# A one-core decoder step: the groups' combination issued in two parts, and the sample's convolution ten taps at a time

## The chip, the cores and the metric

One core of a Trainium2 chip runs one launch. The metric is the device time of the launch in microseconds, the median of several runs. Five engines work side by side, each through its own queue in order: TensorE (PE, with its weight loads listed as PEld), VectorE (DVE), ScalarE (ACT), GpSimd (POOL) and SyncE (SP, which here only issues DMA transfers).

## The reference, cut to what matters

One layer for 1024 prompt tokens and 64 sample tokens (8 sequences of 8), with shared weights, all in float32:

```
h = x @ w_in + b_in                       # 1088 x 10240: conv value, conv gate, silu gates, q, k, v, merge gates
u = a_val * sigmoid(a_gate)               # 1024 channels
conv_raw[t] = sum_j conv_w[j] * u_hist[t + j]     # depthwise, 31 taps; u_hist starts with zeros (prompt)
                                                  # or with 30 stored columns per sequence (sample)
for g in 3 groups (window, dilation) = (128,1), (512,4), (2048,16):   # 8 heads of 64
    o_g, lse_g = dilated window attention with a distance penalty
attn = sum_g softmax_g(lse)[g] * o_g      # "the combination of the groups"
y = LayerNorm(ALPHA * x + W_out(sig(g_a) * W_a(swish(LN(conv_raw)) * silu(z_a)) + sig(g_b) * W_b(attn * silu(z_b))))
```

It also returns the new key, value and convolution buffers.

## The kernel before, in words

Each float32 matrix product is done as three products of high and low parts; `split` (L119 to L122) makes the parts of a weight row block on ACT (hi) and DVE (lo). Products come in chunks of 384, 352 and 352 columns (`proj_chunk`, L192), in one of three PSUM buffers named `mm`. The projection chunks are the bulk of PE's work.

Between them stand the attention *visits*. There are 12 units (f, g): a pair of heads f = 0..3 and a group g = 0..2; a unit is 4, 3 or 2 bursts, one burst a visit. In a visit PE does the transposes of the burst before (L386), the values of the burst before that (L410) and the scores of its own (L357). After the scores DVE adds the penalty and takes the row's extreme (L367), ACT takes the exponentials (L374), and the transposes of the next visit need these. `VISITS` says after how many projection chunks each visit comes. `tc.issue_after(done[0].ins)` puts PE's instructions of a block behind the last projection product traced so far; other engines' instructions in the block are not bound by it.

When the three units of a pair f are done, `combine(f, res)` (L451) joins them: two small POOL transfers bring the row statistics of groups 1 and 2 back (L455), some fifteen DVE operations on 128x16 and one ACT exponential give the weights `w` (L464 to L476); PE transposes `w` (L478), ACT copies it out of PSUM (L480), POOL writes it to DRAM (`wd`, L482) and reads it back spread over 64 partitions each (`wb`, six transfers, L487); then DVE multiplies the three outputs with `wb` and adds them (L489 to L492, five operations of 128x1024). For f = 0, 1, 2 this is called in one piece after the second visit of the next pair (g == 0, bi == 1); for f = 3 in the sample stage, after the first group of sample scores.

The convolution runs channel block by channel block (128 channels, c = 0..7; 0 to 4 beside the attention, 5 to 7 beside the sample stage). `conv_channels(c)` loads 30 stored columns per sequence into a sample buffer `us` (8 sequences x 38 columns; three such buffers take turns, c % 3), projects gate and value, and writes the gated product behind the stored columns (L520 on ACT, L525 on DVE), the prompt's into `ub` (two buffers, c % 2). `conv` then runs the 31 taps on DVE at low priority (LP): for each tap one operation of 128x1024 on the prompt (L541, L544) and one of 128x64 on the sample (L542, L546), both summed in place in one tile `acc` (slot 23, a single buffer), which goes to DRAM (`cvd`, L548). So ACT's write into `ub` of channel c waits for the last prompt tap of channel c-2.

The order of each engine's instructions is written at build time by a list planner: it goes by priority (visits +700, weight splits +1500, convolution -800, otherwise program order) and by its own estimate of when an instruction's inputs are there. At run time each engine follows that order and waits where an input is late.

Of the kernel before, what the change touches and what calls it, by code (L numbers as in the profile page):

```python
# [16 lines left out]
P = 128  # L17
# [3 lines left out]
NS = 64  # L21
# [23 lines left out]
def trunk_kernel(ctx, tc, I, O):  # L45
# [18 lines left out]
    def slot(i, shape, dt=F32, n="s"):  # L64
        return sp.tile(shape, dt, tag=f"S{i}", name=nm(n))
# [14 lines left out]
    def pt_ps():  # L80
        return psm.tile([P, 512], F32, tag="PT", bufs=2, name=nm("PT"))
# [369 lines left out]
    def combine(f, res):  # L451
        stn = tiny.tile([P, 3, 8, 4], F32, tag="stn", bufs=1, name=nm("stn"))
        dve.tensor_copy(out=stn[:, 0].rearrange("p t x -> p (t x)"), in_=res[0][1].rearrange("p t h x -> p (t h x)"))
        for g in (1, 2):
            pool.dma_start(out=stn[:, g], in_=res[g][1].rearrange("(t p) x -> p t x", p=P))  # L455

        nmax = stn.rearrange("p g t (h x) -> p g t h x", x=2)[:, :, :, :, 0]
        lsum = stn.rearrange("p g t (h x) -> p g t h x", x=2)[:, :, :, :, 1]
        mn = tiny.tile([P, 8, 2], F32, tag="mn", name=nm("mn"))
        e = tiny.tile([P, 3, 8, 2], F32, tag="e", bufs=1, name=nm("e"))  # L460
        el = tiny.tile([P, 3, 8, 2], F32, tag="el", bufs=1, name=nm("el"))
        den = tiny.tile([P, 8, 2], F32, tag="den", name=nm("den"))
        w = tiny.tile([P, 3, 2, 8], F32, tag="w", name=nm("w"))
        dve.tensor_tensor(out=mn, in0=nmax[:, 0], in1=nmax[:, 1], op=ALU.min)  # L464
        dve.tensor_tensor(out=mn, in0=mn, in1=nmax[:, 2], op=ALU.min)  # L465
        for g in range(3):
            dve.tensor_tensor(out=e[:, g], in0=mn, in1=nmax[:, g], op=ALU.subtract)
        ef = e.rearrange("p g t h -> p (g t h)")
        act.activation(out=ef, in_=ef, func=AF.Exp)
        for g in range(3):  # L470
            dve.tensor_tensor(out=el[:, g], in0=e[:, g], in1=lsum[:, g], op=ALU.mult)
        dve.tensor_tensor(out=den, in0=el[:, 0], in1=el[:, 1], op=ALU.add)
        dve.tensor_tensor(out=den, in0=den, in1=el[:, 2], op=ALU.add)
        dve.reciprocal(out=den, in_=den)
        for g in range(3):
            dve.tensor_tensor(out=w[:, g].rearrange("p h t -> p t h"), in0=e[:, g], in1=den, op=ALU.mult)  # L476
        pw = pt_ps()
        pe.transpose(pw[:48, :P], w.rearrange("p g h t -> p (g h t)"), ident)  # L478
        wt = half("PT", [48, P], 2)
        act.activation(out=wt, in_=pw[:48, :P], func=AF.Copy)  # L480
        wd = dram.tile([3, 2, NP_], F32, name=nm("wd"))
        pool.dma_start(out=wd.rearrange("g h (t p) -> (g h t) p", p=P), in_=wt)  # L482
        at = attn[f]
        for g in range(3):
            wb = slot(rotate("W", (12, 13)), [P, NP_], n="wb")
            for h in range(2):
                pool.dma_start(out=wb[64 * h:64 * h + 64, :], in_=wd[g, h:h + 1, :].to_broadcast([64, NP_]))  # L487
            if g == 0:
                dve.tensor_tensor(out=at[:, :NP_], in0=res[g][0], in1=wb, op=ALU.mult)  # L489
            else:  # L490
                dve.tensor_tensor(out=wb, in0=res[g][0], in1=wb, op=ALU.mult)
                dve.tensor_tensor(out=at[:, :NP_], in0=at[:, :NP_], in1=wb, op=ALU.add)  # L492


    PAD = 30
# [2 lines left out]
    def conv_channels(c):  # L498

        ub = slot(21 + c % 2, [P, PAD + NP_], n="ub")  # L500
        us = usv[c % 3]
        pool.memset(ub[:, :PAD], 0.0)
        sync.dma_start(out=us[:, :, :PAD], in_=I["state_conv"][c])
        wg = load_w(I["w_in"][F_AGATE + c], D)
        wv = load_w(I["w_in"][F_AVAL + c], D)
        b = b_sb[:, F_AVAL + c:F_AVAL + c + 1]
        bg = b_sb[:, F_AGATE + c:F_AGATE + c + 1]

        def spans(c0, cn):

            n = min(cn, NP_ - c0)
            out = [(slice(0, n), ub[:, PAD + c0:PAD + c0 + n], lambda a: a)]
            if n < cn:
                out.append((slice(n, cn), us[:, :, PAD:], lambda a: a.rearrange("p (b t) -> p b t", b=8)))
            return out

        for c0, cn in CHUNKS:
            ps = proj_chunk([(*wg, xhi, xlo)], c0, cn)
            for sl, dst, view in spans(c0, cn):
                act.activation(out=dst, in_=view(ps[:, sl]), func=AF.Sigmoid, bias=bg)  # L520
            yield
        for c0, cn in CHUNKS:
            ps = proj_chunk([(*wv, xhi, xlo)], c0, cn)
            for sl, dst, view in spans(c0, cn):
                dve.scalar_tensor_tensor(out=dst, in0=view(ps[:, sl]), scalar=b, in1=dst, op0=ALU.add, op1=ALU.mult)  # L525
            if c0 + cn < NT:
                yield
        pool.dma_start(out=O["convp"][c], in_=ub[:, NP_:])
        pool.dma_start(out=O["convs"][c], in_=us[:, :, 8:])
        with tc.high_priority(LP):  # L530
            conv(c, ub, us)
        yield

    def conv(c, ub, us):
        acc = slot(23, [P, NT], n="cv")
        accs = acc[:, NP_:].rearrange("p (b t) -> p b t", b=8)
        for j in range(31):
            w = convw[:, c, j:j + 1]
            if j == 0:
                cb = convb[:, c:c + 1]  # L540
                dve.tensor_scalar(out=acc[:, :NP_], in0=ub[:, :NP_], scalar1=w, scalar2=cb, op0=ALU.mult, op1=ALU.add)  # L541
                dve.tensor_scalar(out=accs, in0=us[:, :, :8], scalar1=w, scalar2=cb, op0=ALU.mult, op1=ALU.add)  # L542
            else:
                dve.scalar_tensor_tensor(out=acc[:, :NP_], in0=ub[:, j:j + NP_], scalar=w, in1=acc[:, :NP_],  # L544
                                         op0=ALU.mult, op1=ALU.add)
                dve.scalar_tensor_tensor(out=accs, in0=us[:, :, j:j + 8], scalar=w, in1=accs,  # L546
                                         op0=ALU.mult, op1=ALU.add)
        pool.dma_start(out=cvd[c], in_=acc)  # L548


    snew = dram.tile([3, 8, NS, NS], F32, name="snew")
# [45 lines left out]
    def beside():  # L597

        for g in range(3):
            yield from project_v(g)  # L600
            if g == 0:
                credit[1] = 1.7
            yield from project_qk(2 + g)
        keep[1] = slot(19, [P, NT], n="keep")
        usv.extend(keep[i][:, c:c + 304].rearrange("p (b t) -> p b t", b=8) for i, c in ((0, 12 * NS), (1, 0), (1, 304)))
        for c in range(5):
            for x in PAIRS[c]:
                yield from project_qk(x)
            yield from conv_channels(c)
# [4 lines left out]
    fill = beside()  # L614
    steps = 0
    n = 0
    for u, (f, g) in enumerate(units):
        if g == 0:
            res = []
        for bi, burst in enumerate(BURSTS[g]):  # L620
            n += 1

            while steps < (VISITS[n - 1] if n <= len(VISITS) else VISITS[-1] + 2.75 * (n - len(VISITS))) or (u not in qk):
                next(fill, None)
                steps += 1
            if bi == 0:
                q, k = qk[u]
                scr = None if g == 0 else dram.tile([NP_, 4], F32, name=nm("scr"))
                un, r = prompt_unit(f, g, q, k, scr)
                res.append(r)  # L630
            elif bi == 1:
                while ("v", g) not in ready:
                    next(fill, None)
                    steps += 1
                un["vt"] = load_v(f, g)
            with tc.issue_after(done[0].ins):
                visit({"unit": un, "tiles": burst})
                if bi == 0:
                    sample_new_scores(f, g, q, k)
            if todo and g == 0 and bi == 1:  # L640
                combine(*todo.pop())
        if g == 2:
            attn[f] = slot(14 + f, [P, NT], n="attn")
            todo.append((f, res))
# [195 lines left out]
    fill = filling()  # L840
    credit[1] = 0.0
    load_tiles()
    new = sample_queries(0)
    for pr in range(4):
        sc = sample_scores(*new)
        if pr < 3:
            new = sample_queries(pr + 1)
        if pr == 0:
            combine(*todo.pop())
            kvs[:0] = [9, 10, 11]  # L850
            odt += [slot(12 + i, [P, 2, 512], n="od") for i in range(2)]
        sample_values(pr, *sc)
# [311 lines left out]
```

## Time and profile before

| | |
|---|---|
| median of three runs | 1428.41 us (1426.35 to 1431.4) |
| the profiled execution | 1428.49 us, span 1426.7 us, clock 0.993 |
| PE busy | 1396.9 us, 98% |
| PEld busy | 1269.5 us, 89% |
| DVE busy | 845.2 us, 59% |
| ACT busy | 442.8 us, 31% |
| POOL busy | 184.6 us, 13% |

Busy times are sums of instruction spans; register, semaphore and DMA-issuing instructions are not counted. "Idle before X <-Y" is the time in which the engine did nothing before instruction X, and Y is what ended last. PEclk is TensorE's clock as a share of full speed.

### The profile page before, as it was taken

What the parts mean: (1) busy time and instruction counts of PE and PEld (TensorE: products, weight loads), DVE (VectorE), ACT (ScalarE), POOL (GpSimd) and SP (SyncE); (2) the same over time, 40 slices, a digit from 0 to 9 for tenths busy, and PEclk for the clock granted to TensorE, in tenths of its full rate; (3) what the DMA queues carried; (4) which work ended last, traced back from release to release, by engine and by line L of the source; (5) the groups of instructions that cost most, each with busy time, mean ns of one, the idle gap of its engine ahead of it and who ended that gap; (6) DMA issues with size and microseconds to landing.
All of it is one profiled execution on the core that took longest, in us unless ns stands there. A gap on an engine that the chain in (4) does not pass through costs nothing.

```text
span 1426.7 us, 21939 instructions
## 1 busy us (share of the span) xinstructions
PE 1396.9 (98%) x8682; PEld 1269.5 (89%) x8682; DVE 845.2 (59%) x1632; ACT 442.8 (31%) x982; POOL 184.6 (13%) x302
## 2 busy tenths in 40 slices
PE   9999999999999999999799999999999999999997
PEld 9989898899999999889587878878899999999886
DVE  4223132433896966968799988581367516335686
ACT  5213132244444353244121212112237423103220
POOL 2010112210111011301641404000000000000000
PEclk9999999999999999999899999999999999999999
DMA  6529285474567466555668687586544436434321
GB/s 235 207 102 337 113 298 210 130 231 172 178 215 217 154 226 201 194 187 134 179 229 275 214 279 273 181 295 249 172 176 174 161 110 219 149 92 147 125 90 74
DMA packets 85110, 271.27 MB, mean 190 GB/s; under 512 B 20912, under 2 KB 40688, under 8 KB 83600
## 3 DMA queue, kind: packets, MB, share of 16 engines
q1 hardware_dynamic: 70704, 147.16, 31.9%
q10 hardware_dynamic: 2816, 87.30, 17.3%
q0 software_dynamic: 11488, 35.42, 7.3%
q8 instruction: 68, 1.11, 0.3%
q14 instruction: 34, 0.28, 0.1%
HBM read 236.39 MB, written 120.74 MB: 250 GB/s over the span
## 4 chain that ended last, share of the span: by engine, by line
PE 86%; DVE 5%; DMA 3%; issue 3%; POOL 2%; ACT 1%; SPq 0%; DVEq 0%; ACTq 0%; POOLq 0%
PE mm L192 59%; PE mm L292 9%; PE mm L1005 7%; DVE cv L544 2%; PE S L357 2%; PE O L410 2%; PE PT L386 2%; PE O L704 2%; PE S L704 1%; POOL qf L722 1%; DMA wb<-wd 1%; DMA scr<-st 1%; PE mm L301 1%; ACT P L374 1%; PE S L738 1%
## 5 line engine op out<-in xcount | busy, mean ns | idle before, releaser
L192 PE MATMUL mm<-x,hi 128*128 128x352 f32 (+1 forms) x3648 | 908.2, 331 | 8.8 <-ACT ub L520 8.5
L192 PEld LDWEIGHTS mm<-x,hi 128*128 128x128 f32 x3648 | 641.8, 189 | 52.8 <-issue 18.5
L192 PE MATMUL mm<-x,lo 128*128 128x352 f32 (+1 forms) x1824 | 597.3, 328 | 0.0
L192 PEld LDWEIGHTS mm<-x,lo 128*128 128x128 f32 x1824 | 343.5, 188 | 1.8 <-issue 1.3
L544 DVE SCALAR_TENSOR_TENSOR cv<-ub,conv_w,cv 128x1024 f32<-128x1024 f32 x240 | 307.9, 1283 | 2.2
L120 ACT ACTIVATE hi<-raw 128x1024 fp32r<-128x1024 f32 (+2 forms) x88 | 86.2, 981 | 281.0 <-PE mm L192 233.4
L121 DVE TENSOR_TENSOR lo<-raw,hi 128x1024 fp32r<-128x1024 f32 (+2 forms) x88 | 99.0, 1126 | 122.7 <-ACT hi L120 122.6
L292 PE MATMUL mm<-vhi,x 128*128 128x512 f32 x384 | 119.9, 391 | 0.0
L374 ACT ACTIVATE P<-P,st 128x128 f32<-128x128 f32 (+1 forms) x192 | 84.6, 442 | 92.1 <-DVE st L367 91.9
L292 PEld LDWEIGHTS mm<-vhi,x 128*128 128x128 f32 x384 | 72.1, 188 | 15.3 <-issue 0.3
L722 POOL COPY qf<-keep 64x16 f32<-64x16 f32 x96 | 71.2, 752 | 43.6 <-PE S L704 40.3
L292 PE MATMUL mm<-vlo,x 128*128 128x512 f32 x192 | 74.7, 389 | 0.0
L293 DVE TENSOR_TENSOR vst<-mm,vb 128x512 f32<-128x512 f32 x24 | 16.6, 691 | 94.9 <-PE mm L292 90.5
L546 DVE SCALAR_TENSOR_TENSOR cv<-keep,conv_w,cv 128x64 f32<-128x64 f32 x240 | 68.7, 286 | 3.4
L825 ACT ACTIVATE gst<-mm,b_in 128x352 f32<-128x352 f32 (+1 forms) x48 | 26.9, 560 | 129.7 <-PE mm L192 90.3
L367 DVE CUSTOM_DVE_ANT_0 P<-S,bias 128x128 f32<-128x128 f32 (+1 forms) x192 | 55.0, 350 | 10.2 <-PE S L357 10.2
L1005 PE MATMUL mm<-wol,mh 128*128 128x512 f32 (+1 forms) x152 | 57.4, 378 | 0.0
L1005 PE MATMUL mm<-woh,mh 128*128 128x512 f32 (+1 forms) x152 | 57.4, 378 | 0.0
L1005 PE MATMUL mm<-woh,ml 128*128 128x512 f32 (+1 forms) x136 | 51.2, 377 | 0.0
L410 PE MATMUL O<-PT,vt 128*64 128x128 f32 x560 | 40.1, 287 | 3.7 <-DVE mn L465 3.7
L292 PEld LDWEIGHTS mm<-vlo,x 128*128 128x128 f32 x192 | 36.1, 188 | 7.3
L386 PE MATMUL PT<-ident,P 128*128 128x128 f32 x280 | 36.5, 273 | 5.5 <-ACT P L374 5.5
(186 smaller groups left out, 1295.3 us busy)
## 6 DMA issues: line engine op xcount, KB each, us to landing
out_nb_dram<-in_cache_dram ACTq DMA_DIRECT2D x64, 1020.0 KB
raw<-in_w_in_dram SPq DMA_DIRECT2D x66, 512.0 KB
kv<-in_g3k_dram SPq DMA_DIRECT2D x32, 512.0 KB
kv<-in_g3v_dram SPq DMA_DIRECT2D x32, 512.0 KB
out_nb_dram<-in_cache_dram ACTq DMA_DIRECT2D x16, 1008.0 KB
kv<-in_g2k_dram SPq DMA_DIRECT2D x16, 512.0 KB
kv<-in_g2v_dram SPq DMA_DIRECT2D x16, 512.0 KB
raw<-in_w_v_dram SPq DMA_DIRECT2D x12, 512.0 KB
```

The costliest lines, as they stand in the source:

```text
L120: h = act.activation(out=dst_hi, in_=src, func=AF.Copy)
L121: dve.tensor_tensor(out=dst_lo, in0=src, in1=dst_hi.bitcast(F32), op=ALU.subtract)
L192: done[0] = pe.matmul(ps[:, :cn], a, b, start=(i == 0), stop=(i == len(ops) - 1))
L292: done[0] = pe.matmul(ps, a, b, start=(i == 0), stop=(i == len(ops) - 1))
L367: dve.tensor_tensor_reduce(out=pr[:, h, c], in0=ps[:, h, c], in1=un["bias"][:, h, b0:b0 + nk], scale=-1.0, scalar=3e38, op0=ALU.add, op1=A ...
L374: x["exp"] = act.activation(out=pr[:, h, c], in_=pr[:, h, c], func=AF.Exp, scale=-1.0, bias=st[:, t, h, 0:1], accum_out=st[:, t, h, 1:2])
L386: m = pe.transpose(pp[:, i * P:(i + 1) * P], x["pr"][:, h, c:c + P], ident)
L410: m = pe.matmul(po[64 * h:64 * h + 64, oc], vt[:, vb[j], 64 * h:64 * h + 64], x["pts"][:, place[t, h, j]], start=(j == 0), stop=(j == nb - 1))
L544: dve.scalar_tensor_tensor(out=acc[:, :NP_], in0=ub[:, j:j + NP_], scalar=w, in1=acc[:, :NP_], op0=ALU.mult, op1=ALU.add)
L546: dve.scalar_tensor_tensor(out=accs, in0=us[:, :, j:j + 8], scalar=w, in1=accs, op0=ALU.mult, op1=ALU.add)
L722: pool.tensor_copy(out=qfull(g)[hs, f].rearrange("p (r j h) -> p r j h", r=4, j=4)[:, :, :, 2 * f + h2], in_=qs[hs, g * 4 + f, 16 * pr:16 ...
L1005: pe.matmul(ps[:, :cn], a, b, start=(j == 0), stop=(j == len(ops) - 1))
```

## The change: what it does, and the diff

`combine` becomes a generator in two parts: up to `w`, and from PE's transpose on. For f = 0 to 2 the first part stays after the second visit, the second part comes after the fourth, its PE transpose behind the last projection product. For f = 3 the first part stands ahead of the first sample queries, the second where the whole stood.

The sample's convolution leaves `conv`: `conv_sample` multiplies overlapping windows of ten taps at once (128x640 products), sums each ten with one reduction, and adds; the 31st tap is one more operation. It has one buffer for the products and two for the sums, in the space of the third `us`; two `us` buffers take turns. The prompt's `acc` shrinks to 1024 columns, and the sample's sums go to DRAM in a transfer of their own.

```diff
@@ combine
         for g in range(3):
             dve.tensor_tensor(out=w[:, g].rearrange("p h t -> p t h"), in0=e[:, g], in1=den, op=ALU.mult)
+        yield
         pw = pt_ps()
         pe.transpose(pw[:48, :P], w.rearrange("p g h t -> p (g h t)"), ident)
...
                 dve.tensor_tensor(out=at[:, :NP_], in0=at[:, :NP_], in1=wb, op=ALU.add)
+        yield
@@ conv_channels
-        us = usv[c % 3]
+        us = usv[c % 2]
...
         with tc.high_priority(LP):
+            conv_sample(c, us)
             conv(c, ub, us)
@@ conv
-        acc = slot(23, [P, NT], n="cv")
-        accs = acc[:, NP_:].rearrange("p (b t) -> p b t", b=8)
+        acc = slot(23, [P, NP_], n="cv")
...
-                dve.scalar_tensor_tensor(out=accs, in0=us[:, :, j:j + 8], scalar=w, in1=accs,
-                                         op0=ALU.mult, op1=ALU.add)
-        pool.dma_start(out=cvd[c], in_=acc)
+        pool.dma_start(out=cvd[c, :, :NP_], in_=acc)
+
+    def conv_sample(c, us):
+
+        prods, sums, more = keep[1][:, 304:944], keep[1][:, 944:1008], keep[1][:, 1008:1072]
+        jn = 10
+        for j0 in (0, 10, 20):
+            win = us[:, :, j0:j0 + 8]
+            win = bass.AP(win.tensor, win.offset, [list(x) for x in win.ap] + [[1, jn]])
+            w = convw[:, c, j0:j0 + jn].unsqueeze(1).unsqueeze(1).to_broadcast([P, 8, 8, jn])
+            dve.tensor_tensor(out=prods.rearrange("p (b t j) -> p b t j", b=8, t=8), in0=win, in1=w, op=ALU.mult)
+            dve.tensor_reduce(out=more if j0 else sums, in_=prods.rearrange("p (x j) -> p x j", j=jn), axis=AX.X,
+                              op=ALU.add)
+            if j0:
+                dve.scalar_tensor_tensor(out=sums, in0=more, scalar=convb[:, c:c + 1] if j0 == 20 else 0.0, in1=sums,
+                                         op0=ALU.add, op1=ALU.add)
+        last = sums.rearrange("p (b t) -> p b t", b=8)
+        dve.scalar_tensor_tensor(out=last, in0=us[:, :, 30:], scalar=convw[:, c, 30:], in1=last, op0=ALU.mult, op1=ALU.add)
+        pool.dma_start(out=cvd[c, :, NP_:], in_=sums)
@@ the unit loop
             if todo and g == 0 and bi == 1:
-                combine(*todo.pop())
+                weights = combine(*todo.pop())
+                next(weights)
+            if weights and g == 0 and bi == 3:
+                with tc.issue_after(done[0].ins):
+                    next(weights)
+                weights = None
@@ the sample stage
     load_tiles()
+    weights = combine(*todo.pop())
+    next(weights)
     new = sample_queries(0)
...
         if pr == 0:
-            combine(*todo.pop())
+            with tc.issue_after(done[0].ins):
+                next(weights)
```

## Rows read from the trace of the kernel before

**Rows 1.** Timeline of PE: start us, us, engine, line, operation, count, idle before.

```profile
579.45 1.09 PE L386 MATMUL PT<-ident,P 128*128 128x128 f32 x8 [1.64 <-ACT P L374]
...
609.68 1.09 PE L386 MATMUL PT<-ident,P 128*128 128x128 f32 x8 [3.91 <-ACT P L374]
...
679.49 1.98 PE L410 MATMUL O<-PT,vt 128*64 128x128 f32 x16 [3.65 <-DVE mn L465]
...
704.24 1.01 PE L192 MATMUL mm<-x,hi 128*128 128x384 f32 x2 [8.50 <-ACT ub L520]
```

**Rows 2.** Windows: busy us of PE, PEld, DVE, ACT, POOL; PEclk; DMA share; GB/s.

```profile
609.00:614.00 5.00, 4.32 (x32) 3.40 (x32) 4.89 (x6) 3.69 (x10) 0.57 (x2) 0.70 1.14 418
...
704.00:709.00 5.00, 4.76 (x15) 4.77 (x16) 0.00 (x0) 1.23 (x4) 2.71 (x6) 0.50 0.61 152
```

**Rows 3.** Timeline of DVE around combine(2).

```profile
569.31 1.23 DVE L489 TENSOR_TENSOR attn<-og,wb 128x1024 f32<-128x1024 f32 x1 [7.77 <-DMA wb<-wd]
...
576.85 0.42 DVE L367 CUSTOM_DVE_ANT_0 P<-S,bias 128x256 f32<-128x256 f32 x1
...
606.03 0.28 DVE L367 CUSTOM_DVE_ANT_0 P<-S,bias 128x128 f32<-128x128 f32 x1
```

**Rows 4.** Timeline: PE's weight transpose, DVE's first multiply; f = 1, then 2.

```profile
428.26 0.28 PE L478 MATMUL PT<-ident,w 128*48 128x128 f32 x1
...
438.32 1.23 DVE L489 TENSOR_TENSOR attn<-og,wb 128x1024 f32<-128x1024 f32 x1 [7.56 <-DMA wb<-wd]
...
551.80 0.27 PE L478 MATMUL PT<-ident,w 128*48 128x128 f32 x1
```

**Rows 5.** Timeline: scores, first L367 and transposes of later visits.

```profile
452.01 1.13 PE L357 MATMUL S<-qkv,qkv 64*128 64x256 f32 x8
...
486.47 0.42 DVE L367 CUSTOM_DVE_ANT_0 P<-S,bias 128x256 f32<-128x256 f32 x1
...
491.52 1.03 PE L386 MATMUL PT<-ident,P 128*128 128x128 f32 x8
...
581.50 1.13 PE L357 MATMUL S<-qkv,qkv 64*128 64x256 f32 x8
...
596.50 1.16 PE L357 MATMUL S<-qkv,qkv 64*128 64x128 f32 x16
```

**Rows 6.** Timeline of DVE: sample taps alone, a pair, prompt taps alone.

```profile
620.66 5.42 DVE L546 SCALAR_TENSOR_TENSOR cv<-keep,conv_w,cv 128x64 f32<-128x64 f32 x17
...
650.76 1.29 DVE L544 SCALAR_TENSOR_TENSOR cv<-ub,conv_w,cv 128x1024 f32<-128x1024 f32 x1
...
651.96 0.29 DVE L546 SCALAR_TENSOR_TENSOR cv<-keep,conv_w,cv 128x64 f32<-128x64 f32 x1
...
697.00 5.24 DVE L544 SCALAR_TENSOR_TENSOR cv<-ub,conv_w,cv 128x1024 f32<-128x1024 f32 x4
```

**Rows 7.** DVE's groups by line: names, shapes, count, busy us, mean ns, idle before.

```profile
L546 DVE SCALAR_TENSOR_TENSOR cv<-keep,conv_w,cv 128x64 f32<-128x64 f32 x240 | 68.7, 286 | 3.4
...
L489 DVE TENSOR_TENSOR attn<-og,wb 128x1024 f32<-128x1024 f32 x4 | 4.9, 1226 | 34.0 <-DMA wb<-wd 34.0
...
L920 DVE TENSOR_TENSOR sb<-sb,attn 128x352 f32<-128x352 f32 (+1 forms) x12 | 6.3, 534 | 7.6 <-ACT sb L919 7.6
```

**Rows 8.** Timeline of DVE, ACT and POOL while channel block 3 is summed.

```profile
671.63 0.26 DVE L748 CUSTOM_DVE_ANT_0 sb<-sb,bias 128x96 f32<-128x96 f32 x1 [6.88 <-DMA raw<-in_w_in_dram]
...
685.10 0.18 DVE L472 TENSOR_TENSOR den<-el 128x16 f32<-128x16 f32 x1
685.23 1.28 DVE L544 SCALAR_TENSOR_TENSOR cv<-ub,conv_w,cv 128x1024 f32<-128x1024 f32 x1
686.43 0.18 DVE L473 TENSOR_TENSOR den<-den,el 128x16 f32<-128x16 f32 x1
...
685.32 17.51 POOL L722 COPY qf<-keep 64x16 f32<-64x16 f32 x22
...
702.30 1.28 ACT L520 ACT_TABLE_LOAD   x1 [6.20 <-DVE cv L544]
```

More of the change, by code (lines that the diff above doesn't have):

```diff
@@ L539, in conv @@
             if j == 0:
-                cb = convb[:, c:c + 1]
-                dve.tensor_scalar(out=acc[:, :NP_], in0=ub[:, :NP_], scalar1=w, scalar2=cb, op0=ALU.mult, op1=ALU.add)
-                dve.tensor_scalar(out=accs, in0=us[:, :, :8], scalar1=w, scalar2=cb, op0=ALU.mult, op1=ALU.add)
-            else:
-                dve.scalar_tensor_tensor(out=acc[:, :NP_], in0=ub[:, j:j + NP_], scalar=w, in1=acc[:, :NP_],
-                                         op0=ALU.mult, op1=ALU.add)
-                dve.scalar_tensor_tensor(out=accs, in0=us[:, :, j:j + 8], scalar=w, in1=accs,
-                                         op0=ALU.mult, op1=ALU.add)
-        pool.dma_start(out=cvd[c], in_=acc)
+                dve.tensor_scalar(out=acc, in0=ub[:, :NP_], scalar1=w, scalar2=convb[:, c:c + 1], op0=ALU.mult, op1=ALU.add)
+            else:
+                dve.scalar_tensor_tensor(out=acc, in0=ub[:, j:j + NP_], scalar=w, in1=acc, op0=ALU.mult, op1=ALU.add)
+        pool.dma_start(out=cvd[c, :, :NP_], in_=acc)
[15 more added lines that the diff above has]
+        pool.dma_start(out=cvd[c, :, NP_:], in_=sums)
     snew = dram.tile([3, 8, NS, NS], F32, name="snew")
@@ L604, in beside @@
         keep[1] = slot(19, [P, NT], n="keep")
-        usv.extend(keep[i][:, c:c + 304].rearrange("p (b t) -> p b t", b=8) for i, c in ((0, 12 * NS), (1, 0), (1, 304)))
+        usv.extend(keep[i][:, c:c + 304].rearrange("p (b t) -> p b t", b=8) for i, c in ((0, 12 * NS), (1, 0)))
         for c in range(5):
@@ L640, in trunk_kernel @@
             if todo and g == 0 and bi == 1:
-                combine(*todo.pop())
+                weights = combine(*todo.pop())
[3 more added lines that the diff above has]
+                    next(weights)
+                weights = None
         if g == 2:
```

## Prediction

> **What bounds the kernel now.** The page's first part comes first: PE is busy for 98% of the span, so the most that an edit to DVE, POOL or ACT work can give back is PE's idle time and the time that PE spends at half clock after it. Then the waits of PE, taken from its timeline: four of them lie between 577 and 705 us [rows 1]. Two (1.64 and 3.91 us) are transposes of an attention visit that wait for ACT's exponentials. One (3.65 us) is the last values product. It is listed under a small operation that ended near it; the instruction whose result it needs is DVE's copy of the O bank, which stands shortly before in DVE's queue. The last (8.50 us) is a projection chunk that finds all `mm` buffers full, because ACT cannot write `ub`. The windows right behind two of these waits show the clock [rows 2]: 0.70 of full over 609 to 614 us, and 0.50, the lower of its two levels (1.2 of 2.4 GHz), over 704 to 709 us, both after PE had stood still. That is 5 x 0.30 = 1.5 us and 5 x 0.50 = 2.5 us of lost work.
>
> Next, what makes DVE late. At 569.31 it starts the first multiply of combine(2) after 7.77 us of standing still for the transfer `wb` [rows 3]. Its order is fixed, so all behind it is late: the L367 that the transposes at 579.45 need start at 576.85, those for 609.68 at 606.03. The 8.50 us have another cause: ACT's first instruction for `ub` of channel block 5 (a table load) waits until 702.30 for DVE's last tap of block 3 [rows 8], whose place in `ub` it takes. So both causes are in DVE's queue, and the sums of busy time say nothing about them.
>
> **The combination in two parts.** PE does not wait for its transpose of `w`, neither for f = 1 nor for f = 2: the rows show no idle time before it [rows 4]. So moving the transpose saves PE nothing by itself. What moves with it is DVE's wait for `wb`. From PE's transpose to DVE's multiply takes 438.32 - 428.26 = 10.1 us for f = 1 and 569.31 - 551.80 = 17.5 us for f = 2 [rows 3, 4]. DVE stood still since 561.5, so its order had allowed at most 9.7 us. The rest is how late the queue gets: 0.4 us with the short chain, 7.8 us with the long one, 4.1 us in the middle.
>
> For f = 2 the old place is emptied: 1.64 + 3.91 us of waiting and 1.5 us of clock, together 7.0 us. The new place is behind the scores of 581.50 [rows 5], which come 1.64 us earlier then. The multiply would stand in order at about 591 us, and the next L367 at about 596.0, the end of the scores that started at 596.50 less 1.64. From the first L367 to the transposes takes 609.68 - 606.03 = 3.65 us, and the transposes are due at 609.68 - 3.91 - 1.64 = 604.1. So 4.4 us of lateness cost nothing. The middle chain costs 0, the long one 3.4 us and, at 1.5 us of clock for 3.91 us of waiting, 1.3 us more. I take -7.0 us, between -2.3 and -7.0.
>
> For f = 1 the old place cost PE nothing, as DVE had no taps to do. The new one, behind the scores of 452.01, is amid the taps of block 1. There the L367 at 486.47 belong to transposes at 491.52 [rows 5]. This kind needs 579.45 - 576.85 = 2.6 us, so the slack is 2.45 us. The short chain costs 0, the middle one 1.65 us and with clock 2.3, the long one 5.35 and 7.4. I take +2.3 us, between 0 and 7.4. For f = 0 there are no taps yet, so 0. For f = 3 the second part keeps its place, behind the same POOL copies; 0. The queues that the step is moved past: POOL's seven transfers go two visits later, and POOL is idle for 87% of the span, so nothing waits for them but DVE's multiply itself.
>
> **The sample's taps.** They are 240 operations of 286 ns [rows 7], and look like 70 us. But 23 of the 31 read stored columns alone, run early, and fill time in which DVE has nothing else (17 in a row at 620.66, 0.32 us each [rows 6]); PE waits for none of them. The other 8 alternate with prompt taps. Four prompt taps alone take 5.24 us, 1.31 each; with a sample tap between, the prompt tap is followed after 1.20 us, and the sample tap takes its 0.29 less the same 0.09 of overlap, 0.20. A pair is 1.40, so a sample tap costs 0.09 us, and 8 cost 0.7 us.
>
> A 640-column product is priced from L489 (1226 ns, 1024 columns) and L920 (534 ns, 363 on average) [rows 7]: 1.05 ns a column, 0.82 us, 0.73 of it not overlapped. No row shows a long reduction. Its bounds are the 0.29 us of a 64-column and the 1.23 us of a 1024-column operation; I take the product's 0.82, since it reads the same 640 columns. Per channel block this is 6 x 0.82 + 3 x 0.29 = 5.8 us in place of 8.9, 25 us in all, none of it on PE's path as long as DVE has idle time around it.
>
> It counts where block 3's taps run to 702.30. The last third of block 3 (a product, a reduction, two small ones) takes 2 x 0.73 + 2 x 0.20 = 1.9 us, less 0.11 for each of the four gaps that it fills: 1.4, so +0.7 over before. In addition the sample sums no longer share `acc`, so block 4's nine operations can run there too, though not before block 3's, as the buffers of products and sums are single. They take 6 x 0.73 + 3 x 0.20 - 9 x 0.11 = 4.0 us. The planner does fill such gaps with work of low priority: a prompt tap stands between L472 and L473, which depend on each other [rows 8]. So the bounds are +0.7 and +4.7 us (+5.3 with block 5's first product; half a microsecond either way for the reductions), and I take +3.5, on the side of the row. It goes to PE one to one, since 704.24 follows from 702.30.
>
> The Trainium skill advises to minimize the number of DVE operations, since each pays a pipeline drain that chaining does not remove (VectorE: DVE Perf Modes, sections "The DRAIN you can't avoid" and "Rules for kernel authors"). Read so, a 64-column tap costs its whole 0.29 us; the pair in [rows 6] shows 0.09, and no run here tests the rule further yet.
>
> **Smaller edits.** Eight more POOL transfers hide in POOL's idle time, with one exception below. Two `us` buffers in place of three make the load of stored columns wait for block c-2. `ub` binds the block to c-2 already; if that cover were gone, SP would hold back weight loads, at most by a transfer's lateness, 7.8 us.
>
> **Sum.** 1428.49 us (the profiled execution, 0.08 above the median shown) - 7.0 + 2.3 + 3.5 = 1427.3, so 1427. This is no change that can be told: a measurement of this kernel separates about 0.3%, 4.3 us. The terms' bounds give 1422.2 to 1438.9.
>
> **Rivals.**
>
> *Sample taps at full price.* If a tap in the chain costs its 0.29 us, 8 cost 2.3 us, and the new 2 x 0.82 + 2 x 0.29 = 2.2; if block 4's operations also stay out of the chain, the third term is 0 and the time 1423.8. With a short chain for f = 1 it is 1421.5. Against it: the pair's spacing. This is also where the skill's rule would lead. Chance 0.25.
>
> *The tap chain of block 3 loses a wait.* DVE stands still for 6.88 us before L748 [rows 8], amid this chain, for a transfer. The first part of combine(3) now stands ahead in program order and may push L748 behind the landing. Then 704.24 comes 6.9 us earlier, the 2.5 us of clock go, and the time is 1427.3 - 9.4 = 1418. Against it: L748 becomes ready as before. Chance 0.12.
>
> *The wait only moves (the change does not do what it says).* With the long chain at both places the terms are -2.3 and +7.4; with +0.7 for the taps 1434. For it: DVE waits for `wb` in every combination, 34.0 us in four [rows 7]. It decides from a chain of about 15 us. Chance 0.14.
>
> *The sums wait behind POOL's copies.* This ends slower. POOL is busy from 685.32 for 17.51 us with 22 copies, to 702.83 [rows 8]. The transfer of block 4's sums, if it stands behind them, lands about 4 us later (two transfers and a copy fit into 10.1 us), near 707. Block 5's first reduction may not overwrite the sums before. If it stands ahead of block 3's last taps, these end near 708 or later, not at 702.30: in place of +3.5 the term is +6 to +12, and the time 1430 to 1436, middle 1433. It decides once block 4's sample operations end before 702. Chance 0.16.
>
> **Chances and range.** The forecast has the remaining 0.33. Faster by more than 0.3% are the first two rivals, 0.37; slower the last two, 0.30; within it 0.33. From 1415 to 1438 the range takes in the first rivals nearly whole and the term bounds but for their ends.
>
> **What would show it.** Right: no wait of PE near 579 and 609; L489 for f = 1 and 2 about 30 us later, still after several microseconds of idle DVE; a small wait near 491; the wait for ACT's `ub` near 704 longer by some 3 us, with 640-column operations between block 3's taps. Wrong: this wait gone or halved, no products among these taps, or a DVE wait for the sums' transfer.

## The result, and the profile after

The changed kernel takes 1439.03 us (median of six runs, 1435.79 to 1439.88) against 1428.29 us before: a ratio of 1.0069, interval 1.0054 to 1.0084, slower. The forecast was 1427 with a range up to 1438; the time lies just above it. The profiled execution has a span of 1436.9 us, 10.2 more than before, at a clock of 0.988.

The timeline of PE after, its waits of 0.4 us and more between 580 and 720 us, answers to [rows 1]:

```profile
584.97 0.29 PE L479 MATMUL PT<-ident,w 128*48 128x128 f32 x1 [0.45 <-DVE PT L394]
...
611.51 1.97 PE L386 MATMUL PT<-ident,P 128*128 128x128 f32 x8 [4.43 <-ACT P L374]
...
681.50 1.09 PE L410 MATMUL O<-PT,vt 128*64 128x128 f32 x16 [1.64 <-DVE mn L465]
698.46 1.93 PE L725 MATMUL S<-kv,qf 128*32 128x512 f32 x8 [4.24 <-POOL qf L743]
716.56 1.01 PE L192 MATMUL mm<-x,hi 128*128 128x384 f32 x2 [16.17 <-ACT ub L522]
```

The wait at 579 is gone, the one at 609 is not (4.43 against 3.91 us), and the wait for `ub` has nearly doubled, from 8.50 to 16.17 us. The windows of after, then the same ones of before (busy us of PE, PEld, DVE, ACT, POOL; clock; DMA share; GB/s):

```profile
600.00:625.00 25.00, 20.57 (x121) 18.80 (x120) 19.64 (x39) 10.12 (x32) 8.97 (x15) 0.86 0.78 237
...
700.00:725.00 25.00, 8.83 (x45) 7.35 (x42) 20.17 (x20) 2.91 (x5) 2.26 (x6) 0.60 0.25 88
```

```profile
600.00:625.00 25.00, 21.09 (x133) 19.48 (x132) 20.08 (x51) 10.78 (x33) 1.20 (x3) 0.93 0.60 193
...
700.00:725.00 25.00, 19.46 (x118) 17.12 (x122) 16.76 (x20) 3.97 (x6) 13.40 (x19) 0.80 0.76 251
```

In the second window PE works 8.83 us in place of 19.46, and the granted clock falls with it, to 0.60. The whole loss lies before 725 us. At the chunk that waits for `ub` PE is 12.3 us behind before (716.56 against 704.24), and at the end 10.2.

Now the timeline of DVE while block 3 is summed (the answer to [rows 8]): the first tap, the first and last products (L555) and reductions (L556) of the sample amid its taps, and the two waits.

```profile
646.36 0.80 DVE L542 TENSOR_SCALAR cv<-ub,conv_w,conv_b 128x1024 f32<-128x1024 f32 x1
647.08 0.82 DVE L555 TENSOR_TENSOR keep<-keep,conv_w 128x640 f32<-128x640 f32 x1
...
650.15 0.81 DVE L556 TENSOR_REDUCE keep<-keep 128x64 f32<-128x640 f32 x1
...
675.48 0.26 DVE L769 CUSTOM_DVE_ANT_0 sb<-sb,bias 128x96 f32<-128x96 f32 x1 [4.38 <-DMA bias<-in_nbias_dram]
...
700.95 0.82 DVE L556 TENSOR_REDUCE keep<-keep 128x64 f32<-128x640 f32 x1 [3.09 <-DMA cvd<-keep]
...
704.02 0.82 DVE L555 TENSOR_TENSOR keep<-keep,conv_w 128x640 f32<-128x640 f32 x1
...
705.95 0.81 DVE L556 TENSOR_REDUCE keep<-keep 128x64 f32<-128x640 f32 x1
```

And POOL, then ACT, in the same stretch:

```profile
686.14 12.32 POOL L743 COPY qf<-keep 64x16 f32<-64x16 f32 x20
698.40 0.56 POOL L563 DMA_DIRECT2D cvd<-keep  x1
```

```profile
714.63 1.28 ACT L522 ACT_TABLE_LOAD   x1 [19.44 <-DVE cv L544]
```

From its first tap to the end of its last, block 3 now takes 68.2 us (646.36 to 714.57) against 59.4 (642.85 to 702.24). Between them stand 6 products (4.92 us), 6 reductions (4.88) and 6 small operations (1.48): the last third of block 3, all of block 4, and two thirds of block 5. That is 11.28 us of work in place of 2.30 for the eight old taps. The waits add 0.6 (3.09 + 4.38 - 6.88), and about 0.8 us comes back by overlap. The wait of 3.09 us is that of block 5's first reduction for the transfer of block 4's sums, which POOL issued at 698.40, behind 20 copies.

### The profile page after: what moved, and what is told of

Read it like the earlier page. It is cut to its first block, busy times and chain, and to the rows that moved or that the text cites. A ratio compares the mean times of both kernels' runs of the same rounds, so it can differ in the third digit from the quotient of the medians.

```text
span 1436.9 us, 21782 instructions
## 1 busy us (share of the span) xinstructions
PE 1397.9 (97%) x8682; PEld 1269.5 (88%) x8682; DVE 831.5 (58%) x1456; ACT 442.4 (31%) x982; POOL 182.2 (13%) x310
## 4 chain that ended last, share of the span: by engine, by line
PE 87%; issue 4%; DMA 3%; DVE 3%; POOL 2%; ACT 1%; SPq 0%; DVEq 0%; ACTq 0%; POOLq 0%
PE mm L192 59%; PE mm L292 9%; PE mm L1029 7%; PE S L357 2%; PE O L410 2%; PE O L725 2%; PE PT L386 2%; PE S L725 1%; DVE cv L544 1%; POOL qf L743 1%; PE mm L301 1%; DMA stn<-scr 1%; DMA wb<-wd 1%; PE S L759 1%; PE O L804 1%
## 5 line engine op out<-in xcount | busy, mean ns | idle before, releaser
L743 POOL COPY qf<-keep 64x16 f32<-64x16 f32 x96 | 64.9, 688 | 53.5 <-PE S L725 50.4
L367 DVE CUSTOM_DVE_ANT_0 P<-S,bias 128x128 f32<-128x128 f32 (+1 forms) x192 | 54.9, 345 | 9.9 <-PE S L357 9.9
L394 DVE COPY PT<-PT 128x512 f32<-128x512 f32 x36 | 24.6, 684 | 56.5 <-PE PT L386 56.5
L357 PE MATMUL S<-qkv,qkv 64*128 64x128 f32 (+1 forms) x384 | 41.3, 345 | 0.0
```

The lines of the kernel that those rows point to most:

```text
L357: m = pe.matmul(ps[:, h, off[t]:off[t] + nb * P], q[hs, qc], k[hs, kc], start=True, stop=True)
L367: dve.tensor_tensor_reduce(out=pr[:, h, c], in0=ps[:, h, c], in1=un["bias"][:, h, b0:b0 + nk], scale=-1.0, scalar=3e38, op0=ALU.add, op1=A ...
L743: pool.tensor_copy(out=qfull(g)[hs, f].rearrange("p (r j h) -> p r j h", r=4, j=4)[:, :, :, 2 * f + h2], in_=qs[hs, g * 4 + f, 16 * pr:16 ...
```

## The experiments

All ratios are to the kernel before, with a 95% interval. Beside the experiments before had medians of 1429.55 to 1433.34 us, against 1428.29 in the result; so compare the ratios, and take a time in us as good to some 5 us. "Chain" is block 3's stretch from the first prompt tap to the end of the last, "ub" PE's wait for ACT's `ub` there, both from the profile.

| kernel | ratio | chain, us | ub, us |
|---|---|---|---|
| before | 1 | 59.4 | 8.50 |
| after | 1.0069 (1.0054 to 1.0084) | 68.2 | 16.17 |
| E1 combination alone | 0.9982 (0.9965 to 0.9999) | 55.9 | 7.57 |
| E2 ten taps alone | 1.0105 (1.0085 to 1.0126) | 75.8 | 24.28 |
| E3 after, sample behind | 0.9936 (0.9914 to 0.9959) | 57.1 | 6.67 |
| E4 after, two sums | 1.0000 (0.9984 to 1.0016) | 69.2 | 16.36 |
| E5 before, bias behind | 0.9997 (0.9981 to 1.0012) | 57.2 | 9.59 |
| E6 E3 + bias behind | 0.9941 (0.9920 to 0.9963) | 57.1 | 9.05 |
| E7 after, one tap | 0.9949 (0.9930 to 0.9968) | 58.0 | 6.43 |
| E8 E2, sample behind | 0.9995 (0.9984 to 1.0006) | 57.8 | 6.89 |
| E9 E6 + maxima | 0.9913 (0.9887 to 0.9940) | 55.8 | 8.65 |
| E10 E9 + products | 0.9930 (0.9908 to 0.9952) | 55.8 | 8.43 |
| E11 after, blocks 3 to 5 behind | 0.9900 (0.9879 to 0.9920) | 57.2 | 7.17 |
| E12 E3 with single taps | 0.9986 (0.9967 to 1.0005) | 57.9 | 7.53 |
| E13 after, copies moved | 1.0005 (0.9990 to 1.0021) | 70.4 | 19.23 |
| E14 after, products later | 1.0026 (1.0000 to 1.0053) | 69.0 | 16.86 |
| E15 E11, no waits | 0.9887 (0.9863 to 0.9910) | 52.6 | 7.08 |
| E16 before, no waits | 0.9932 (0.9908 to 0.9955) | 52.6 | 7.08 |
| E17 E15 + E14 | 0.9878 (0.9851 to 0.9905) | 52.6 | 7.08 |
| E18 E15 + E13 | 0.9877 (0.9848 to 0.9906) | 52.6 | 7.08 |

### Which part costs, and by what: E1, E2, E3, E8, E7

E1 is before with the diff of `combine` and its callers alone; E2 is before with the diff of the convolution alone. E3 is after, and E8 is E2, with

```diff
-            conv_sample(c, us)
-            conv(c, ub, us)
+            last = conv(c, ub, us)          # returns its last prompt tap
+            with tc.issue_after(last.ins):
+                conv_sample(c, us)
```

E7 keeps the place of the change and leaves out 30 of the sample's 31 taps: `conv_sample` is its last tap and the transfer.

> The combination in two parts alone, the convolution as before. Theory (block 3's chain of taps took in the sample's operations of blocks 3, 4 and 5, and that is the loss): this kernel is not slower than before, 1424 to 1429 us; PE's wait at 579.45 for DVE (3.91 us) is gone, the one near 610 stays at 3.5 to 4.5 us, the one at 704.24 for ACT's ub stays at 8 to 9 us. Rival (the combination's second part is what costs, by taking VectorE and ScalarE in the two visits where the exponentials stand): 1433 to 1439 us, with the loss near 600 or in the stretch 700 to 725.

> The ten-tap form of the sample's convolution alone, the combination as before. Theory: slower than before by most of the whole change, 1436 to 1443 us; PE's wait for ACT's ub near 716 is 15 to 18 us against 8.50 before. Rival (the combination costs): within 0.3% of before, 1424 to 1432 us, and the wait at 8 to 10 us.

> The changed kernel with each block's sample operations issued behind that block's last prompt tap. Theory: what costs is their place inside block 3's chain of taps; the wait for ACT's ub falls from 16.17 us to 6 to 10 us and the kernel comes to 1427 to 1432 us. Rival (their number and size costs wherever they stand, or it is the combination): 1436 to 1440 us.

> The sample's convolution ten taps at a time and behind the last prompt tap, with the combination in one part as before. Theory (place, not the combination): 1422 to 1429 us, near the kernel that has the combination in two parts as well. Rival (the two-part combination is what made that one faster than before): 1430 to 1436 us.

> The changed kernel with only one of the sample's 31 taps computed (one small operation and its transfer per block, at the same place; the output of the sample's convolution is left incomplete), to price all that the sample's operations cost where they stand. Theory: block 3's chain falls from 68.2 us to 53 to 56 us, PE's wait from 16.17 to 5 to 9 us, the wait of 4.43 us near 611 shrinks too: 1420 to 1427 us. Rival (half of the loss is the combination's second part): 1431 to 1435 us.

The combination costs nothing (E1, at the edge of a small gain; its stalls are at 483 and 557 us, 3.07 and 3.98 us, and not at 610 as expected), and the ten taps alone cost more than the whole change and more than expected (E2, 1448.18 us). In E2 the undivided combination(3) puts five of its operations of 128x1024, and a wait of 1.61 us ahead of them, into the same chain; 75.8 us is its length, 24.28 us PE's wait. Put behind the last prompt tap, the same operations cost nothing that shows: E8 against E2 is 0.9995 against 1.0105, E3 against after 0.9936 against 1.0069, and E3 is no slower than E7 (0.9949), which leaves nearly all of them out. PE's wait for `ub` in E2, then E3:

```profile
727.11 1.01 PE L192 MATMUL mm<-x,hi 128*128 128x384 f32 x2 [24.28 <-ACT ub L520]
```

```profile
698.82 1.01 PE L192 MATMUL mm<-x,hi 128*128 128x384 f32 x2 [6.67 <-ACT ub L522]
```

E3 came below its expectation (1423.66 us): the stall near 610 was gone there too, which the theory had not said. E8 kept stalls of 2.80 and 1.04 us near 584 and 613. Its time lies in the theory's range, but it is no faster than before and E3 is: so what made E3 faster than before is the combination in two parts, as the rival had it, worth 0.6% once the sample's operations are out of the way. E7 gives what those operations cost where the change has them: 1421.09 us against 1439.03, 0.9949 against 1.0069; part of it is the stall near 611, which shrank to 2.63 us. Its chain is longer than expected (58.0 us, not 53 to 56); its time is as expected.

### What the sums' wait is worth: E4

```diff
-        ..., sums, ... = ..., keep[1][:, 944:1008], ...
+        sums = keep[1][:, 944:1008] if c % 2 == 0 else keep[2][:, 1024:1088]
```

> The changed kernel with a second buffer for the sample's sums, used by the odd blocks, so that a block's first reduction no longer waits for the transfer of the block before. Theory: the two waits of 2.27 and 3.09 us are gone, PE's wait for ACT's ub falls by about 3 us to 13 us, 1435 to 1437 us. Rival A (the waiting transfer behind POOL's copies is the whole loss): 1427 to 1431 us. Rival B (the wait is covered by another): 1438 to 1440 us.

Both waits for the sums' transfer are gone, and the kernel is 0.7% faster than after, more than expected, but not where expected: PE's wait for `ub` stays at 16.36 us. There the wait for the bias table grew to 8.48 us, which ate what the sums' wait gave:

```profile
669.12 0.26 DVE L770 CUSTOM_DVE_ANT_0 sb<-sb,bias 128x96 f32<-128x96 f32 x1 [8.48 <-DMA raw<-in_w_in_dram]
```

The gain is the stall near 611, gone with the half clock behind it: block 3's chain begins at 637.40 us, 9.0 earlier than after, and ends at 706.63, 7.9 earlier, and the span is 7.5 us shorter. The wait of 4.24 us for POOL's copy at 698 is gone too, but behind it PE stands for `ub` in either kernel. So the theory's place was wrong and rival B's right; its time was neither's.

### Is it the place or the form, and which blocks: E12, E11

E12 is E3 with the 31 single taps of before in `conv_sample`; E11 is after with the edit of E3 for blocks 3, 4 and 5 only.

> The changed kernel with the sample's 31 taps one at a time, as before the change, but in a run of their own behind the block's last prompt tap. Theory (the place decides and not the form): block 3's chain is near 52 to 58 us, 1421 to 1428 us, within 0.3% of the ten-tap form at that place. Rival (the ten-tap form is what pays): 1430 to 1438 us.

> The changed kernel with the sample's operations behind the last prompt tap for blocks 3, 4 and 5 alone, whose operations stood inside block 3's chain; those of blocks 0 to 2 stay where the change has them. Theory: PE's wait for ub falls from 16.17 us to 6 to 10 us; the wait for the sums' transfer in block 2 stays, and with it some of the stall near 611; 1425 to 1432 us. Rival (the place of the sample's operations matters in every block alike): 1433 to 1438 us.

E12's chain is as expected (57.9 us, E3's is 57.1), its time is not: 1430.39 us lies in the rival's range, and 0.9986 against E3's 0.9936 is a difference that the intervals part. E12 has stalls of 1.93, 1.06 and 3.99 us near 437, 552 and 614 that E3 lacks, so the difference lies outside block 3's chain. The last of them follows the broadcast: DVE waits 4.14 us at 606.47 for its last part, which landed 12.7 us behind its issue. Whether the form brings the rest is not settled, since one profile each shows them. E11 beat both theories: 1418.91 us. PE's wait for `ub` is as expected, but the stall near 611 is gone as well: with block 3's operations late, its first reduction no longer runs into the transfer of block 2's sums, and block 2's chain takes 58.1 us against 71.6 after, with one wait of 1.36 us for the broadcast in place of 2.27 and 5.37.

### Why the stall near 610 stayed: E13, E14 (and E10)

After, ACT issues a pair of cache copies of 1,020 KB each just ahead of POOL's broadcast, and DVE stands for it. ACT, POOL and DVE of after:

```profile
591.69 1.32 ACTq L157 DMA_DIRECT2D out_nb_dram<-in_cache_dram  x2
```

```profile
592.71 2.07 POOL L488 DMA_DIRECT2D wb<-wd  x4 [2.77 <-DMA wd<-PT]
```

```profile
602.49 1.23 DVE L490 TENSOR_TENSOR attn<-og,wb 128x1024 f32<-128x1024 f32 x1 [5.37 <-DMA wb<-wd]
...
607.94 0.28 DVE L367 CUSTOM_DVE_ANT_0 P<-S,bias 128x128 f32<-128x128 f32 x1
```

E13 takes the copies away from it (it issues the pair one call of `pace` earlier), E14 takes the product out of the scores' way:

```diff
@@ E13: pace(), which issues the copies
         credit[0] += credit[1]
+        paced[0] += 1
+        credit[0] += {42: 2.0, 43: -2.0}.get(paced[0], 0.0)
@@ E14: combine() yields once more ahead of the products; the unit loop
+            if weights and g == 1 and bi == 0:
+                with tc.issue_after(scored[0].ins):    # the last L367 of this visit
+                    next(weights)
```

> The changed kernel with one pair of ScalarE's cache copies (1,020 KB each), which was issued 1.02 us ahead of the third combination's broadcast (591.69 against 592.71 us), issued 15 us earlier together with the single copy there. Theory (the broadcast queues behind that pair: in the profiles so far it landed 9.8 to 11.3 us after its issue in the eight kernels where the pair went ahead or within 0.1 us of it, and 4.9 to 6.0 us in four of the five where the pair came at least 0.7 us behind): the first product with it starts 4.5 to 6.5 us after the broadcast's issue, PE's wait of 4.43 us near 611 is gone, 1430 to 1435 us. Rival (something else in the transfers delays it): 9 us and more again, and 1437 to 1441 us.

> The changed kernel with the products with the broadcast weights (L490 to L493) issued on VectorE behind the scores of the next group's first visit (in the kernel with products later, above, they had kept their place on VectorE). Theory (the stall near 611 is VectorE standing at the first product ahead of the scores whose exponentials PE waits for): PE waits less than 1 us there, the wait for ub stays at 15 to 17 us, 1430 to 1435 us. Rival (the wait moves to another operation of that stretch, or the later products lengthen the chain of taps by as much): 1437 to 1441 us.

Both took the stall away: PE is busy for 25.00 of the 25 us from 600 in either, at full clock, and the times are 1433.47 and 1433.93 us, both as the theories had them. E13, then E14:

```profile
600.00:625.00 25.00, 25.00 (x184) 23.83 (x180) 18.51 (x39) 14.62 (x38) 8.01 (x15) 1.00 0.72 234
```

```profile
600.00:625.00 25.00, 25.00 (x180) 23.53 (x179) 18.93 (x46) 14.16 (x38) 5.70 (x14) 1.00 0.83 269
```

E13's profile is of its slowest execution, 1436.02 us; its chain holds waits of 5.54 and 4.33 us. E14's is of its fastest, 1430.25; four of its twelve took 1442.89 to 1446.29 us, which no profile shows. With E11 these two price the place alone, as none of the three has the stall: 1.0005 and 1.0026 with the sample's operations in block 3's chain, 0.9900 with those of blocks 3 to 5 behind their taps.

The transfers of the broadcast in a window of 4 us (line, count, size, median us from issue to landing), after and then E13:

```profile
wb<-wd POOLq DMA_DIRECT2D x4, 256.0 KB, 9.9
```

```profile
wb<-wd POOLq DMA_DIRECT2D x4, 256.0 KB, 4.6
```

The product itself starts without a wait at 602.45, 8.8 us behind the issue, later than expected, as DVE had taps to do until then. E10 (E9 with the third part, but bound to PE's order alone) did not move the products on DVE: they started at 604.19 after 7.98 us of waiting, and its time tells nothing about them (one of its ten executions, 1965.76 us, is left out of the ratio).

> The same with a third part of the combination: the products with the broadcast weights (L490 to L493) are issued in the first visit of the next group, two visits behind the transfers. Theory (the stall near 610 is VectorE standing at the first of these products until the broadcast lands, 4.9 to 10.7 us behind its issue in the profiles so far): no PE wait over 1 us between 570 and 620, and 2 to 6 us faster than the kernel without it: 1412 to 1417 us. Rival (the wait goes to another operation there): no faster than the kernel without it.

### Is block 3's chain the bound: E5, E6, E9, E15, E16

E5 and E6 issue the operation on the bias table (L748 of before) behind the scores of its visit; E9 adds a `yield` ahead of the maxima of `combine`; E15 (from E11) and E16 (from before) bind both to the first sample scores by `tc.issue_after` on a DVE instruction.

```diff
@@ E15, E16: the scores' loop (E5, E6, E9 have m.ins for seen[0].ins)
+            with tc.issue_after(seen[0].ins) if i == 2 else nullcontext():
                 m = dve.tensor_tensor_reduce(out=sx[i], ...)
@@ E15, E16: the second part of combine(3), after sample_scores
+            with tc.issue_after(seen[0].ins):
+                next(weights)
```

> The kernel before, with the one VectorE operation that waits 6.88 us for the small bias table inside block 3's chain of taps (L748) issued behind the operation on the other scores of its visit. Theory (block 3's chain sets when ScalarE may write the next ub, so whatever is taken out of it shortens PE's wait there one for one): the chain falls from 59.4 to 51 to 54 us, PE's wait of 8.50 us for ub to 1 to 4 us, the kernel comes to 1416 to 1424 us. Rival (the transfers and POOL's copies around it end the wait just after): the time stays within 0.3% of before.

> The changed kernel with the sample's operations behind each block's last prompt tap and the operation on the bias table behind the other scores. Theory: block 3's chain falls from 52.1 us to 46 to 48 us and PE's wait for ub from 6.67 us to 0 to 3 us: 1414 to 1420 us. Rival (at this point POOL's copies of the queries, for which PE waited 0.94 us here, become the bound): 1421 to 1425 us.

> The kernel with the sample's operations and the bias operation behind, and beside them the last combination's maxima (which then waited 5.25 us for their transfer inside block 3's chain) issued after the first sample scores. Theory (VectorE's chain of block 3 is the bound and each time an operation that waits for a transfer stands in it, the next one in line takes its place): with none left in it the chain falls from 57.1 to 48 to 52 us and PE's wait for ub from 9.05 to 2 to 5 us: 1415 to 1420 us. Rival (something else ends that wait: POOL's copies or the sample's tiles): 1421 to 1426 us.

> The kernel with the sample's operations of blocks 3 to 5 behind their taps, and the operation on the bias table and the last combination's maxima issued behind the first sample scores, so that no operation that waits for a transfer is left in block 3's chain. Theory (that chain is the bound at 690 us): the chain falls from 57.2 to 46 to 51 us, PE's wait for ub from 7.17 to 0 to 3 us, 1411 to 1416 us. Rival (POOL's copies, the sample's tiles or the freed operations' own lateness take its place): 1417 to 1421 us.

> The kernel before with the same two things issued behind the first sample scores. Theory: block 3's chain falls from 59.4 to 48 to 53 us and PE's wait for ub from 8.50 to 0 to 3 us; the stalls at 579 and 609 us stay: 1418 to 1424 us. Rival: PE waits there for something else, 1427 to 1431 us.

In E5 the wait of 6.88 us is gone and the next one in line took its place; the kernel is no faster, as the rival had it:

```profile
677.81 0.18 DVE L466 TENSOR_TENSOR mn<-mn,stn 128x16 f32<-128x16 f32 x1 [4.64 <-DMA stn<-scr]
```

E6 went the same way: its chain is as long as E3's (57.1 us, not 52.1 as its expectation has it for E3), with 5.25 us at 678.59 in place of 5.41 for the bias table. A stall of 6.50 us came back at 613, in a profile of its slowest execution; its nine times fall into four at 1416.1 to 1417.0 and five at 1422.9 to 1426.7 us. In E9 the maxima kept their place (4.16 us at 676.91), so it is no test of the theory. E15 and E16 have neither wait. E16 came out at 1422.85 us, as the theory had it, and E15 at 1416.14, a little above and not told from E11 (0.9887 against 0.9900). In E16 the chain ends 5.4 us earlier than in before (696.87 against 702.24) and PE goes on 5.4 us earlier (698.86 against 704.24), so the chain is the bound. But in both PE waits 7.08 us for `ub` and not 0 to 3; in E16 PE also comes earlier, as its 3.65 us at 679 are gone. DVE, then ACT, in E15:

```profile
688.51 1.23 DVE L122 TENSOR_TENSOR lo<-raw,hi 128x1024 fp32r<-128x1024 f32 x1 [1.55 <-PE S L733]
689.66 3.92 DVE L550 SCALAR_TENSOR_TENSOR cv<-ub,conv_w,cv 128x1024 f32<-128x1024 f32 x3
```

```profile
687.42 1.06 ACT L121 ACTIVATE hi<-raw 128x1024 fp32r<-128x1024 f32 x1 [12.16 <-PE mm L193]
693.64 1.28 ACT L524 ACT_TABLE_LOAD   x1 [5.16 <-DVE cv L550]
694.94 1.42 ACT L524 ACTIVATE ub<-mm,b_in 128x384 f32<-128x384 f32 x3
```

The last three taps stand behind a weight split (L122) whose high part ACT can make only when PE has ended the product before. (DVE's row names PE's scores; they and the high part both ended at 688.48.) PE's end, the split, three taps, a table load and the first `ub` add up to the 7.08 us, the same in all four kernels without the two waits (E15 to E18), though their chains begin at 637.0 to 644.3 us. This is read from the traces; no run moves the split.

### Both causes away: E17, E18

> The kernel without waits in block 3's chain, with the products with the broadcast weights behind the scores as well. Theory (the two causes are separate and their gains add): PE's wait of 3.32 us at 609 is gone and the kernel is 3 to 5 us faster than without this, a ratio to before of 0.984 to 0.987. Rival (the time gained at 609 is given back at the wait for ub near 695 us, since block 3's chain starts no earlier): 0.988 to 0.991.

> The kernel without waits in block 3's chain, with the pair of cache copies moved ahead by 15 us instead. Theory: as the one above, 0.984 to 0.987. Rival: 0.988 to 0.991.

PE no longer waits at 609 in either (25.00 us busy from 600), and the profiled spans are 1411.1 and 1412.1 us against 1415.7 for E15. The medians are 1415.07 and 1414.70 us; the ratios lie between the two expectations, and their intervals take in E15's. Whether the two prices add in full is not settled. These two are the fastest here, 1.2% below before.

## Why the prediction was wrong

**The third term, +3.5 us, was too small, and is the loss.** The prices of the operations were right: the products take 819 ns and the reductions 812 ns in the mean, against 0.82 assumed for both.

```profile
L555 DVE TENSOR_TENSOR keep<-keep,conv_w 128x640 f32<-128x640 f32 x24 | 19.7, 819 | 1.8 <-PE mm L301 1.8
L556 DVE TENSOR_REDUCE keep<-keep 128x64 f32<-128x640 f32 x24 | 19.5, 812 | 5.5 <-DMA cvd<-keep 5.4
```

What failed is the count. The step let block 4's operations into the chain, with one product of block 5 at most; block 5's came too, as far as its second third, with the sums' wait amid them. The term measured is +8.8 us of chain (68.2 - 59.4), and PE's wait grew by 7.67. The other 3.5 of the 12.3 us that PE is late there are the chain's later start (646.36 against 642.85); 1.8 of these are there at 105 us, long before the first tap (362.7 us) and the first combination, and the remaining 1.7 stand against the -4.7 of the first two terms. E2 with E8, after with E3, and E13 and E14 with E11 show the place as the cause. The mechanism is that of the rival "the sums wait behind POOL's copies", down to the late reduction at 700.95; but its range, +6 to +12, is met more by the operations themselves (9.0 us more work) than by its wait: E4, which takes the wait away, leaves PE's wait for `ub` as it was.

**The first term, -7.0 us, failed.** Two waits and 1.75 us of clock (25 us at 0.93) made 7.3 us before; 0.45 + 4.43 us and 3.5 us of clock make 8.4 after. The step said that the long chain, transposes to product, would cost 4.7 us at the new place, and took none. The chain was the long one, 17.5 us (584.97 to 602.49), for two reasons: ACT's copy of the weights came at 588.85, behind an exponential that had waited, and the broadcast took 9.9 us to land. Also, block 2's chain, ahead of it in the queue, held a wait of 2.27 us for the sums' transfer at 562.69. E13 and E14 each take the stall away by one edit. E4 and E11 lost the sums' wait and the stall as well, but there the broadcast also went ahead of the copies by 0.7 us, so the part of the sums' wait in it is not shown alone. The term's bound with the long chain was -2.3, and it came to +1.1; for the sums' wait ahead of it, 2.27 us, the step had no place. The gain itself is real where it can show: the combination in two parts is worth 0.6% in E3 against E8.

**The second term, +2.3 us, was 0.** For f = 1 the chain was of middle length, 456.67 to 470.39, 13.7 us, and no wait of PE followed near 491; the term lies within its bounds.

**The other rivals.** "Sample taps at full price" needed block 4's operations out of the chain; they were in it. "The tap chain loses a wait" is out for the changed kernel (4.38 us of the 6.88 stayed), and E5 shows that it would have brought nothing: its 1418 counted a wait as gained that the next one in the queue takes over. "The wait only moves" was near the truth for f = 2, and wrong for f = 1.

**Fewer operations.** E8 has the sample's convolution in 72 operations, where before has 248, and is no faster (0.9995); after is slower. The place differs as well, though, and at one place, behind the last prompt tap, E12's 248 are slower than E3's 72 (0.9986 against 0.9936); 4 of the 7.6 us between those two profiles are the stall at 614, which follows the broadcast. So these runs neither bear out nor refute the advice of the Trainium skill that the prediction weighed, to keep the number of operations down (VectorE: DVE Perf Modes, "Rules for kernel authors").

## What to carry to other kernels

Work of low priority that a planner drops into gaps of a chain is free only while the chain has slack: bind it behind the chain's last instruction, and bind it by an instruction of the same engine's queue. Before counting a wait as gained, look for the next instruction in that queue that waits, and for the one after it. A transfer that an engine stands waiting for should be issued ahead of bulk copies on other queues, or the copies paced around it.

## What was not expected of the hardware

The landing of the broadcast for f = 2 (four transfers of 256 KB) hangs on where ACT's pair of cache copies is issued. In the ten profiles where the pair went ahead of it or within 0.1 us, the median from issue to landing was 9.6 to 10.7 us; with no pair for at least 2.6 us after (E1, E13, E18) it was 4.6 to 4.8; with the pair 1.9 us behind 6.1 (E3). Between, 0.6 to 0.9 us behind, it was 7.2 to 7.8 in three kernels (E4, E11, E12) and 10.2 to 10.7 in three others (E7, E15, E17). DVE's first product needs the first two of the four transfers: in E4, E11 and E12 the second of them was issued 0.2 us ahead of the pair and landed after 4.3 to 4.5 us; in E15 and E17 it was less than 0.1 us ahead and landed after 9.6 to 10.0. E7 does not fit (0.4 us ahead, 9.3 us), so something else has a part in it. The Trainium skill says that transfers started by different engines end up on the same 16 DMA engines and interleave (DMA: Bandwidth & Descriptors, "Issuing engines are not separate DMA queues"); these rows agree, and show that which was issued first counts. E3 and E6 have the same instructions around 610 us: in E3's profile the pair came 1.9 us behind the broadcast and DVE stood 2.02 us for the first product, in E6's it came 0.25 us ahead and DVE stood 9.04, and only E6 shows the stall. That this order brings the stall is what E13 tests; whether it also parts E6's two groups of times no run shows.
